# Letting the tile scheduler order three engines in the dense stages of a two-layer hybrid step, with kept output weights and a two-deep chain of sums

## The chip, the cores and the metric

The kernel runs on one core of a Trainium2 chip. The metric is the device time of one execution in microseconds (us). TensorE (PE) multiplies, VectorE (DVE) and ScalarE (ACT) do the elementwise work, GpSimd (POOL) some sums, and SyncE (SP) issues most DMAs.

## The reference, cut to what matters

One inference step over 1024 latent tokens and 256 context tokens, width 1024, in two layers. Layer 0 mixes tokens with a bidirectional S5 scan, layer 1 with grouped-query attention; a SwiGLU FFN of inner width 2816 follows each.

```
for layer in range(2):
    h = modulate(x, shift1, scale1)
    m = s5_mixer(h) if layer == 0 else attention(h)      # s5: scan, gelu, GLU, w_out; attention: qkv, softmax, w_o
    x = layer_norm(ALPHA * x + gate1 * m)
    h = modulate(x, shift2, scale2)
    f = (silu(h @ w_gate) * (h @ w_up)) @ w_out
    x = layer_norm(ALPHA * x + gate2 * f)
```

All arithmetic keeps fp32 accuracy.

## The kernel before

**Layout.** Activations lie feature-major: 8 feature tiles of 128 rows, with the tokens in three chunks: c=0 and c=1 of 512 latent tokens, c=2 of 256 context tokens. Nearly everything lies in one pool of 88 pages of 128x512 fp32 (and 12 half pages).

**Split products.** A matrix product is three matmuls: each fp32 operand is split into a high part (a rounding copy on ScalarE) and a low part (a subtraction on VectorE), and high-high, high-low and low-high are accumulated in PSUM. Weights come by SP's DMA into three raw buffers (`wr`) and are split a half tile at a time (`w_ahead`, lines 102 and 103; for the gated products `i_step`, lines 914, 919 and 923).

**Gated products** (`ffn_step`): the S5 GLU (8 tiles) and the FFN inputs (22 tiles in each layer). The two latent chunks are treated as a 2x2 block product in Winograd's way with 7 block products P1 to P7, each of 12 matmuls of 128x512 (line 961). They need differences of the input h: T1, T2, T3, T4 (`x_next`: a subtraction on line 852, the high part on 855, the low part on 856), and the plain splits B11, B21, B22 (lines 830 and 831). G and U are the context chunk's products, 24 matmuls of 128x256 each (line 971). A *head* of a tile is what needs only chunk 0 (P1, P2) and chunk 2 (G, U); a *tail* is the rest. Five tiles of each gated product start as heads, because chunk 0 is normalised first; their tails follow. P1 ends in a ScalarE copy (line 977), P2 in a VectorE add (981) and the activation (982). The result is spilled to DRAM.

**Output products** (`out_chunks`): 8 output tiles f, contracted over nk=8 tiles (S5 output, attention output w_o) or nk=22 (FFN output), in passes over chunks. `TWO` is first chunks 0 and 2 and then chunk 1; `ONE`, only after the last FFN, is chunk 0, chunk 1, chunk 2. Weights are loaded and split anew in each pass. VectorE accumulates (line 631). In the last pass's f=7 a list of hooks prepares the next stage.

**Boundary** (`cross`, `boundary`, `layer_norm`): the layer norm of a chunk is a generator that yields estimated durations (`YW`). `boundary` weaves its steps by an estimated clock between the units of matmul work: first the output pass of the next chunks, then the heads. A factor `YS`=1.4 stretches the steps, so that they come later. A layer norm subtracts the mean (line 698), squares on ScalarE (700), sums the 8 squares with 7 VectorE adds (702 and 706), sums over features by a matmul with a column of ones (711), takes a reciprocal square root on VectorE, spreads it (691), multiplies (718), makes the modulated h (727) and the residual (752), which ScalarE's own DMA queue stores. After chunk 1's layer norm come, still in the boundary, all of T1, T2, T3, T4 and B22 (`x_rest`), one after the other.

**Order of the instructions.** Everything stands under `tc.manual_schedule()`: each engine issues its instructions in the order in which the Python code emits them. Without it, the tile framework's scheduler would pick, for each engine, the order by simulating the program: of the instructions that are ready at a simulated moment it takes the one that was emitted first. Either way the order is fixed at build time and each engine works through its own list.

Of the kernel before, what the change touches and what calls it, by code (L numbers as in the profile page):

```python
# [6 lines left out]
F32 = mybir.dt.float32  # L7
# [8 lines left out]
KT = 8  # L16
# [597 lines left out]
class Dense(S5):  # L614
# [63 lines left out]

    def layer_norm(self, acc, c, cols, raw, ready, after=None, then=()):

# [16 lines left out]
        for kt in range(KT):  # L697
            v.tensor_tensor(acc[kt][c], acc[kt][c], pm, op=ALU.subtract)
            q[kt] = self.pgn(n)
            nc.scalar.activation(q[kt], acc[kt][c], AF.Square)  # L700
            if kt > 2:
                v.tensor_tensor(q[0], q[0], q.pop(kt - 2), op=ALU.add)
            if kt in (2, 5):
                yield YW[1] * n / 512
        for kt in range(KT - 2, KT):
            v.tensor_tensor(q[0], q[0], q.pop(kt), op=ALU.add)
        yield YW[2] * n / 512 + YW[3]

        ps = self.psum()
        for t in range(nt):  # L710
            mm(ps[:, t:t + 1], q[0][:, 128 * t:128 * t + 128], self.ones[:, 0:1], start=True, stop=True)
        rstd = self.small.tile([P, 4], F32, tag="rstd", name=self.nm("rstd"))[:, :nt]
# [42 lines left out]

    def boundary(self, outs, passes, ln, heads, ready, slow=1.0):

        gens = []
        self.rs = {}
        clock = [0.0, 0.0]  # L760

        def step():
            t = next(gens[0], None)
            if t is None:
                gens.pop(0)
                t = YW[0]
            return t * slow

        def run(units):

            for u in units:
                clock[0] += u() or 0.0
                while gens and clock[0] >= clock[1]:
                    clock[1] = max(clock[1], clock[0] - 2.0) + step()

        for units, cs in zip(outs, passes):
            run(units)
            if not gens:
                clock[1] = clock[0] + YW[0]
            gens += [ln(c, ready) for c in cs]  # L780
        for c, units in heads or ():
            while not ready[c]:
                clock[1] = clock[0] + step()
            run(units)
        lap = 0
        while gens:

            for g in [gens[-1]] * (2 if lap == 3 else 1) + gens[-2::-1]:
                if next(g, 0) == 0:
                    gens.remove(g)  # L790
            lap += 1
# [17 lines left out]

YT, YS = 1.8, 1.4  # L810

# [3 lines left out]
class Ffn(Dense):  # L815

    def x_start(self, raw):
        self.xr = raw
        self.hs = {}
        self.X = {n: [None] * 4 for n in ("B11", "B21", "B22", "T1", "T2", "T3", "T4")}  # L820
        self.xt = {}
        self.xq = {"B11": 0, "B21": 0, "B22": 0, "T1": 0, "T2": 0, "T3": 0, "T4": 0, "C": 0}
# [11 lines left out]
    def x_next(self, n):  # L834

        nc, r = self.nc, self.xr
        v = nc.vector
        k = self.xq[n]
        if k == (8 if n == "C" else 4):
            return False  # L840
        self.xq[n] += 1
        if n == "C":
            self.h_split(k, 2, v)
        elif n[0] == "B":
            kt, c = k + 4 * (n[1] == "2"), int(n[2]) - 1
            self.h_split(kt, c, v)
            self.X[n][k] = self.hs[kt, c]
        else:
            t = self.page()
            x, y = {"T1": lambda: (r[k][1], r[k][0]), "T2": lambda: (r[k + 4][1], self.xt["T1", k]),  # L850
                    "T3": lambda: (r[k + 4][1], r[k][1]), "T4": lambda: (r[k + 4][0], self.xt["T2", k])}[n]()
            v.tensor_tensor(t, x, y, op=ALU.subtract)
            self.xt[n, k] = t
            hi, lo = self.page(F32R), self.page(F32R)
            nc.scalar.activation(hi, t, AF.Copy)
            v.tensor_tensor(lo, t, hi.bitcast(F32), op=ALU.subtract)
            self.X[n][k] = hi, lo
        return True

    def x_all(self, *names):  # L860
        for n in names:
            while self.x_next(n):
                pass

    def x_rest(self, *names):

        for n in names or ("T1", "T2", "T3", "T4", "B22"):
            while self.x_next(n):
                yield YT


# [66 lines left out]
    def ffn_step(self, i, kind, act):  # L938
# [39 lines left out]
        elif kind == "P2":  # L978
            B = product("B", True)
            x = e["s1"] = self.page() if head else e["s1"]  # L980
            v.tensor_tensor(x, e["s2"] if head else x, B, op=ALU.add)
            ac(x, x, act)
        elif kind == "P5":
# [51 lines left out]
    def ffn_body(self, act, last):  # L1035
        for i in range(self.nhead, len(self.segs)):
            for s, kind in enumerate(self.segs[i][1][1]):
                if i == len(self.segs) - 1:
                    last(s)
                self.ffn_step(i, kind, act)  # L1040
        self.X = self.hs = self.xr = self.xt = self.ev = None

# [37 lines left out]

    def out_chunks(self, acc, gate, nk, passes, residual, scale=None, hook=()):

# [9 lines left out]
        def unit(p, f, lo):  # L1092
            cs = passes[p]
            hi = min(lo + 8, nk)
            if lo == 0:
                st["ps"] = [self.psum()[:, :CH[c][1]] for c in cs]
                for c in cs:
                    if f == 0:
                        load(c, 0)
                    if f < 7:  # L1100
                        load(c, f + 1)
            w = self.w_next()
            base = sum(nk * len(x) for x in passes[:p])
# [391 lines left out]


NHP = 12, 88

# [3 lines left out]
class Full(Attn):  # L1502
    def run(self):
        tc, nc, I = self.tc, self.nc, self.I
        with ExitStack() as st:
            st.enter_context(tc.manual_schedule())
            dp = st.enter_context(tc.tile_pool(name="dram", bufs=1, space=bass.MemoryType.DRAM))
# [20 lines left out]
            self.pages.release()  # L1528
            self.pp.release()

    def rows(self, n, *ix):
        return [self.I[n][ix + (i,)] for i in range(self.I[n].shape[len(ix)])]

    def rest(self):
# [30 lines left out]


        self.wpools.append(tc.alloc_tile_pool(name="w2", bufs=1, side="left", reuse_waits="tile"))
        zz = new()
# [25 lines left out]
        self.out_start(KT, TWO, self.spilled)  # L1594
        self.wseq += self.out_plan(L("w_s5_out"), KT, 2)
        self.LS = 1.5
# [7 lines left out]
        def ffn(l, cols, outs, acc, passes):  # L1604

            raw = self.xr
            self.cross(outs, TWO, acc, cols, raw, ready, self.ffn_heads(AF.Silu), keep, self.x_rest())
            self.out_start(NF, passes, self.spilled)
# [8 lines left out]

        outs = lambda: self.out_chunks(acc, self.mod(0, 2), KT, TWO, inputs, ALPHA, ffn_hook(0))

# [26 lines left out]
        acc = None  # L1646
        self.LS = 2
        self.at_queries(hh, hl)
        hh = hl = self.hs = self.xr = None
        self.wseq += self.out_plan(L("w_o"), KT, 2)  # L1650
        self.LS = 1.5
# [3 lines left out]
        ahead.update({(2 + k // 3, 2 * (k % 3)): [lambda k=k: self.z_ahead(2 * k + 2, 0)] for k in range(6)})  # L1655
        self.attention(ahead)
        self.apool.release()
        acc = new()
        hook = ffn_hook(1)
        outs = self.out_chunks(acc, self.mod(1, 2), KT, TWO, self.residual, None, hook)  # L1660

# [6 lines left out]
    def cross(self, outs, passes, acc, cols, raw, ready, heads, after, then=()):  # L1668
        ready[:] = [False] * 3
        self.boundary(outs, passes, lambda c, ready: self.layer_norm(acc, c, cols, raw, ready, after, then if c == 1 else ()),  # L1670
                      heads, ready, YS if then else 1.0)

# [367 lines left out]
```

## Time and profile before

| | |
|---|---|
| median of 3 runs | 3472.22 us (3468.31 to 3476.12) |
| the profiled execution | 3475.9 us, span 3474.1 us |
| PE busy | 3198.7 us, 92% |
| DVE, ACT, POOL busy | 2109.9 us, 1401.9 us, 274.5 us |
| mean granted TensorE clock | 0.957 of full |

Busy is the time in which an engine has an instruction at work. Matmuls are pipelined, so the duration of one is longer than the time from one to the next. The clock is the share of full speed that was granted to TensorE. The span is the time from the first to the last instruction of the core; the time of a run also holds what lies around it.

### The profile page before, as it was taken

What the parts mean: (1) busy time and instruction counts of PE and PEld (TensorE: products, weight loads), DVE (VectorE), ACT (ScalarE), POOL (GpSimd) and SP (SyncE); (2) the same over time, 40 slices, a digit from 0 to 9 for tenths busy, and PEclk for the clock granted to TensorE, in tenths of its full rate; (3) what the DMA queues carried; (4) which work ended last, traced back from release to release, by engine and by line L of the source; (5) the groups of instructions that cost most, each with busy time, mean ns of one, the idle gap of its engine ahead of it and who ended that gap; (6) DMA issues with size and microseconds to landing.
All of it is one profiled execution on the core that took longest, in us unless ns stands there. A gap on an engine that the chain in (4) does not pass through costs nothing. (4 is left out here: it accounts for less than half of the span.)

```text
span 3474.1 us, 46877 instructions
## 1 busy us (share of the span) xinstructions
PE 3198.7 (92%) x17674; PEld 2675.3 (77%) x17674; DVE 2109.9 (61%) x4381; ACT 1401.9 (40%) x2740; POOL 274.5 (8%) x286
## 2 busy tenths in 40 slices
PE   8989659997699999999989999999859999999997
PEld 5753648886478888888878899998647888888776
DVE  7899646556664444524566888885666444453645
ACT  3351433336422222413543577773552222232433
POOL 1230100010000000010012310001000000000001
PEclk9999779998799999999999999999879999999998
DMA  7679942343122121624421100103322222244544
GB/s 257 171 222 323 239 126 85 100 153 114 65 83 77 61 78 61 205 65 139 140 93 57 61 21 16 35 1 101 106 72 85 75 73 66 73 156 133 172 126 137
DMA packets 229971, 384.04 MB, mean 111 GB/s; under 512 B 54688, under 2 KB 111296, under 8 KB 228976
## 3 DMA queue, kind: packets, MB, share of 16 engines
q1 hardware_dynamic: 208720, 335.12, 30.7%
q0 software_dynamic: 7632, 25.35, 2.4%
q10 hardware_dynamic: 13392, 20.58, 1.6%
q8 instruction: 138, 2.26, 0.3%
q14 instruction: 89, 0.73, 0.1%
HBM read 300.23 MB, written 80.74 MB: 110 GB/s over the span
## 5 line engine op out<-in xcount | busy, mean ns | idle before, releaser
L961 PE MATMUL ps<-pg,pg 128*128 128x512 f32 x4368 | 1050.4, 399 | 121.3 <-ACT pg L919 61.7
L961 PEld LDWEIGHTS ps<-pg,pg 128*128 128x128 f32 x4368 | 830.2, 192 | 310.6 <-ACT pg L919 71.8
L121 PE MATMUL ps<-pg,pg 128*128 128x512 f32 (+1 forms) x1872 | 641.5, 365 | 37.6 <-ACT pg L131 17.4
L123 PE MATMUL ps<-pg,pg 128*128 128x512 f32 (+1 forms) x1872 | 634.5, 361 | 4.1 <-DVE pg L132 3.6
L125 PE MATMUL ps<-pg,pg 128*128 128x512 f32 (+1 forms) x1872 | 629.6, 359 | 0.2 <-DVE pg L103 0.2
L121 PEld LDWEIGHTS ps<-pg,pg 128*128 128x128 f32 x1872 | 350.2, 192 | 103.8 <-ACT pg L131 22.2
L123 PEld LDWEIGHTS ps<-pg,pg 128*128 128x128 f32 x1872 | 350.1, 192 | 63.4 <-DVE pg L132 9.9
L125 PEld LDWEIGHTS ps<-pg,pg 128*128 128x128 f32 x1872 | 349.2, 191 | 54.1 <-DVE pg L103 2.1
L971 PEld LDWEIGHTS ps<-pg,pg 128*128 128x128 f32 x2496 | 318.7, 195 | 23.8 <-ACT pg L830 14.4
L971 PE MATMUL ps<-pg,pg 128*128 128x256 f32 x2496 | 322.1, 286 | 14.8 <-ACT pg L830 13.8
L102 ACT ACTIVATE pg<-wr 128x512 fp32r<-128x512 f32 x344 | 191.8, 597 | 356.4 <-DMA wr<-in_w_ffn_out 163.8
L103 DVE TENSOR_TENSOR pg<-wr,pg 128x512 fp32r<-128x512 f32 x344 | 259.1, 793 | 125.8 <-ACT pg L102 114.4
L631 DVE SCALAR_TENSOR_TENSOR pg<-ps,mods,pg 128x512 f32<-128x512 f32 x64 | 47.9, 749 | 274.0 <-PE ps L125 269.4
L923 DVE TENSOR_TENSOR pg<-wr,pg 128x512 fp32r<-128x512 f32 x232 | 158.1, 685 | 41.9 <-ACT pg L919 41.9
L132 DVE TENSOR_TENSOR pg<-ps,pg 128x512 fp32r<-128x512 f32 (+1 forms) x210 | 141.8, 676 | 62.1 <-ACT pg L131 56.8
L919 ACT ACTIVATE pg<-pg 128x512 fp32r<-128x512 f32 x208 | 129.8, 625 | 119.3 <-DVE pg L914 110.7
L1126 POOL TENSOR_TENSOR pg<-pg,pg 128x512 f32<-128x512 f32 x8 | 10.6, 1330 | 1863.4 <-DVE pg L631 1119.7
L1376 ACT ACTIVATE pg<-ps,nb,rq 128x512 f32<-128x512 f32 x192 | 148.9, 777 | 5.4 <-DVE sm L1385 2.4
L131 ACT ACTIVATE pg<-ps 128x512 fp32r<-128x512 f32 (+1 forms) x210 | 123.8, 591 | 65.9 <-PE ps L1396 47.6
L919 ACT ACTIVATE pg<-wr 128x512 fp32r<-128x512 f32 x232 | 137.6, 620 | 28.2 <-DMA wr<-in_w_s_glu 14.7
L923 DVE TENSOR_TENSOR pg<-pg,pg 128x512 fp32r<-128x512 f32 x208 | 142.3, 685 | 0.2
L1015 ACT ACTIVATE pg<-pg 128x512 f32<-128x512 f32 x52 | 32.9, 632 | 262.6 <-DVE pg L1014 262.6
(337 smaller groups left out, 4543.1 us busy)
## 6 DMA issues: line engine op xcount, KB each, us to landing
wr<-in_w_ffn_in SPq DMA_DIRECT2D x104, 512.0 KB, 3.6
gw<-in_w_mod SPq DMA_DIRECT2D x192, 256.0 KB, 5.1
wr<-in_w_ffn_out SPq DMA_DIRECT2D x80, 512.0 KB, 3.9
dI<-pg SPq DMA_DIRECT2D x104, 256.0 KB, 4.6
pg<-dI SPq DMA_DIRECT2D x104, 256.0 KB, 5.2
wr<-in_w_ffn_out SPq DMA_DIRECT2D x40, 384.0 KB, 3.9
dX<-pg ACTq DMA_DIRECT2D x48, 256.0 KB, 2.0
pg<-dX SPq DMA_DIRECT2D x48, 256.0 KB, 4.0
```

Source lines behind the costliest of these rows:

```text
L102: nc.scalar.activation(hi, x, AF.Copy)
L103: nc.vector.tensor_tensor(lo, x, hi.bitcast(F32), op=ALU.subtract)
L121: mm(ps[c], wh, rh[c], start=first, stop=False)
L123: mm(ps[c], wh, rl[c], start=False, stop=False)
L125: mm(ps[c], wl, rh[c], start=False, stop=last)
L131: self.nc.scalar.activation(hi, src, AF.Copy)
L132: self.nc.vector.tensor_tensor(lo, src, hi.bitcast(F32), op=ALU.subtract)
L919: nc.scalar.activation(hi, self.isum[i, name], AF.Copy)
L923: v.tensor_tensor(lo, self.isum[i, name], hi.bitcast(F32), op=ALU.subtract)
L961: mm(e[bank], p[:, o], q, start=(first and k == 0 and j == 0), stop=(k == 3 and j == 2), skip_group_check=True)
L971: mm(ps, p[:, o], q, start=(k == 0 and j == 0), stop=(k == KT - 1 and j == 2))
L1376: nc.scalar.activation(p, u["bank"].pop((qt, kc)), AF.Exp, bias=nb[:, 0:1], scale=rq, accum_out=sm[:, kc:kc + 1])
```

## The change

The whole mixer of layer 0 (with the scan) and the queries and attention of layer 1 stay in the emitted order on every engine. In the other stages only SP and GpSimd keep it; the order of TensorE, VectorE and ScalarE is the scheduler's.

- The output products with nk=8 (S5 output and w_o) load and split their weights once, keep all 8 split tiles (4 pages each) through the first pass, and give them back in the second.
- `x_next` puts off the low part of a T until the next T's subtraction has been emitted. In the FFN boundaries `x_rest` makes only T1 and T2; T3, T4 and B22 are made inside the first tail, after P6, P5 and P7.
- In a head, P2 accumulates in P1's PSUM bank, and the activation reads the bank: the add on line 981 goes for heads.
- `layer_norm` gets `short`: no VectorE adds of squares; TensorE sums all 8 squares with the column of ones (8 accumulating matmuls for each 128 tokens in place of one). It is used for chunk 1 of the two FFN-entry boundaries and for chunk 2 of the last layer norm.
- The stretch factor becomes 0.5 during the output passes and 0.8 during the heads (`YS`), and `YT` goes from 1.8 to 1.4.

```diff
@@ layer_norm
-            q[kt] = self.pgn(n)
+            q[kt] = self.page()[:, :n] if short else self.pgn(n)
...
-            if kt > 2:
+            if kt > 2 and not short:
                 v.tensor_tensor(q[0], q[0], q.pop(kt - 2), op=ALU.add)
...
-            mm(ps[:, t:t + 1], q[0][:, 128 * t:128 * t + 128], self.ones[:, 0:1], start=True, stop=True)
+            for kt in sorted(q):
+                mm(ps[:, t:t + 1], q[kt][:, 128 * t:128 * t + 128], self.ones[:, 0:1], start=(kt == 0), stop=(kt == max(q)))
@@ boundary
-            return t * slow
+            return t * pace[last[0]]
@@
-YT, YS = 1.8, 1.4
+YT, YS = 1.4, (0.5, 0.8)
@@ x_next
-            hi, lo = self.page(F32R), self.page(F32R)
+            self.x_flush()
+            hi = self.page(F32R)
             nc.scalar.activation(hi, t, AF.Copy)
-            v.tensor_tensor(lo, t, hi.bitcast(F32), op=ALU.subtract)
-            self.X[n][k] = hi, lo
+            def rest():
+                lo = self.page(F32R)
+                v.tensor_tensor(lo, t, hi.bitcast(F32), op=ALU.subtract)
+                self.X[n][k] = hi, lo
+            self.xlo.append(rest)
...
+    def x_flush(self):
+        for f in self.xlo:
+            f()
+        self.xlo = []
@@ ffn_step
         elif kind == "P2":
-            B = product("B", True)
-            x = e["s1"] = self.page() if head else e["s1"]
-            v.tensor_tensor(x, e["s2"] if head else x, B, op=ALU.add)
-            ac(x, x, act)
+            if head:
+                e["s1"] = self.page()
+                ac(e["s1"], product("R", False), act)
+            else:
+                x = e["s1"]
+                v.tensor_tensor(x, x, product("B", True), op=ALU.add)
+                ac(x, x, act)
@@ ffn_body
                 self.ffn_step(i, kind, act)
+                if i == self.nhead:
+                    self.x_all(*{"P6": ("T3",), "P5": ("T4",), "P7": ("B22",)}.get(kind, ()))
@@ out_chunks
-            w = self.w_next()
+            if keep and p:
+                w = st.pop(("w", f))
+            else:
+                w = self.w_next()
+                if keep:
+                    st["w", f] = w
@@ run, rest
-            st.enter_context(tc.manual_schedule())
+            self.guard = None
+            self.order()
...
+KEEP = {mybir.EngineType.SP, mybir.EngineType.Pool}
...
+        self.guard = self.tc.manual_schedule(engines=engines) if engines else self.tc.manual_schedule()
...
+        self.order(KEEP)
...
-        self.wseq += self.out_plan(L("w_s5_out"), KT, 2)
+        self.wseq += self.out_plan(L("w_s5_out"), KT, 1)
...
+        self.order()
         self.at_queries(hh, hl)
...
         self.attention(ahead)
+        self.order(KEEP)
@@ cross
-        self.boundary(outs, passes, lambda c, ready: self.layer_norm(acc, c, cols, raw, ready, after, then if c == 1 else ()),
-                      heads, ready, YS if then else 1.0)
+        self.boundary(outs, passes, lambda c, ready: self.layer_norm(acc, c, cols, raw, ready, after, then if c == 1 else (),
+                                                                                    c == passes[-1][0] and (then != () or heads is None)),
+                      heads, ready, YS if then else (1.0, 1.0))
```

## Rows read from the trace of the kernel before

**Rows 1.** The page's busy time, and PEclk by 40 slices.
```profile
PE 3198.7 (92%) x17674; PEld 2675.3 (77%) x17674; DVE 2109.9 (61%) x4381; ACT 1401.9 (40%) x2740; POOL 274.5 (8%) x286
PEclk9999779998799999999999999999879999999998
```

**Rows 2.** Windows: stretch, length; busy PE, PEld, DVE, ACT, POOL; clock; DMA share, GB/s.
```profile
457.36:545.00 87.64, 63.91 (x241) 50.06 (x242) 52.80 (x89) 35.86 (x65) 0.00 (x0) 0.80 0.32 84
768.60:812.40 43.80, 42.02 (x191) 34.19 (x189) 30.81 (x55) 21.36 (x35) 7.77 (x6) 1.00 0.34 116
812.40:931.90 119.50, 67.86 (x317) 54.39 (x317) 78.31 (x161) 71.95 (x129) 0.00 (x0) 0.74 0.24 80
931.90:1437.60 505.70, 499.82 (x2616) 429.97 (x2617) 255.45 (x416) 146.11 (x269) 0.00 (x0) 1.00 0.24 79
...
2481.00:2602.50 121.50, 68.81 (x317) 55.70 (x317) 78.38 (x161) 71.43 (x128) 0.00 (x0) 0.76 0.23 78
...
3236.50:3369.00 132.50, 126.23 (x547) 102.23 (x546) 65.93 (x115) 46.30 (x86) 9.33 (x6) 0.96 0.44 141
3369.00:3452.50 83.50, 68.86 (x522) 67.04 (x520) 50.50 (x97) 36.81 (x69) 5.99 (x6) 0.90 0.52 161
3452.50:3474.10 21.60, 2.88 (x10) 2.16 (x10) 10.87 (x38) 6.13 (x13) 3.44 (x6) 0.62 0.15 49
```

**Rows 3.** The chain that ended last, in FFN 1's body: start, us, what.
```profile
2736.52 13.63 PE ps L961 x60
2750.15 2.87 PE ps L971 x24
```

**Rows 4.** TensorE's timeline at FFN 0's entry: start, us, work [idle before, releaser].
```profile
812.19 0.39 PE L125 MATMUL ps<-pg,pg 128*128 128x512 f32 x1
817.50 1.22 PE L961 MATMUL ps<-pg,pg 128*128 128x512 f32 x2 [4.92 <-ACT pg L919]
...
840.51 1.01 PE L711 MATMUL ps<-ones,hp 128*128 128x1 f32 x4 [3.17 <-DVE hp L706]
...
852.12 8.26 PE L971 MATMUL ps<-pg,pg 128*128 128x256 f32 x48 [6.90 <-ACT pg L830]
...
881.29 1.05 PE L711 MATMUL ps<-ones,pg 128*128 128x1 f32 x8 [0.45 <-DVE pg L706]
...
904.15 12.15 PE L961 MATMUL ps<-pg,pg 128*128 128x512 f32 x24 [16.45 <-ACT pg L855]
931.91 4.63 PE L961 MATMUL ps<-pg,pg 128*128 128x512 f32 x12 [15.61 <-ACT pg L919]
```

**Rows 5.** VectorE's timeline at the same place.
```profile
813.32 4.90 DVE L831 TENSOR_TENSOR pg<-pg,pg 128x512 fp32r<-128x512 f32 x8 [4.03 <-ACT pg L830]
...
832.32 1.08 DVE L698 TENSOR_TENSOR hp<-hp,ps 128x256 f32<-128x256 f32 x3
...
898.16 0.69 DVE L856 TENSOR_TENSOR pg<-pg,pg 128x512 fp32r<-128x512 f32 x1 [0.69 <-ACT pg L855]
...
900.15 0.69 DVE L856 TENSOR_TENSOR pg<-pg,pg 128x512 fp32r<-128x512 f32 x1 [0.70 <-ACT pg L855]
```

**Rows 6.** Weight splits on VectorE in the S5 output's second pass.
```profile
L103 DVE TENSOR_TENSOR pg<-wr,pg 128x512 fp32r<-128x512 f32 x11 | 7.2, 687 | 5.3 <-ACT pg L102 5.3
```

**Rows 7.** Groups by line and shape, whole span: busy us, mean ns | idle before.
```profile
L102 ACT ACTIVATE pg<-wr 128x512 fp32r<-128x512 f32 x304 | 179.0, 622 | 339.4 <-DMA wr<-in_w_ffn_out 163.8 <-PE ps L123 59.8 <-DMA wr<-in_w_o 41.7
...
L981 DVE TENSOR_TENSOR pg<-pg,ps 128x512 f32<-128x512 f32 x52 | 35.7, 687 | 143.4 <-PE ps L961 143.4
...
L977 ACT ACTIVATE pg<-ps 128x512 f32<-128x512 f32 x52 | 30.9, 594 | 80.6 <-PE ps L961 80.4
L702 DVE TENSOR_TENSOR pg<-pg,pg 128x512 f32<-128x512 f32 x40 | 30.4, 759 | 0.1
...
L702 DVE TENSOR_TENSOR hp<-hp,hp 128x256 f32<-128x256 f32 x20 | 8.4, 422 | 0.0
```

**Rows 8.** Line 961 on TensorE at the S5 GLU's start: min/median/max ns.
```profile
L961 PE MATMUL ps<-pg,pg x193: 387/393/795, 457.4 to 545.0; 128*128 128x512 f32 x193
```

More of the change, by code (lines that the diff above doesn't have):

```diff
@@ L677, in rsqrt, with layer_norm @@
             v.scalar_tensor_tensor(out if it == 2 else y, t, 1.5, y, op0=ALU.add, op1=ALU.mult)
-    def layer_norm(self, acc, c, cols, raw, ready, after=None, then=()):
+    def layer_norm(self, acc, c, cols, raw, ready, after=None, then=(), short=False):
         nc = self.nc
@@ L704, in layer_norm @@
                 yield YW[1] * n / 512
-        for kt in range(KT - 2, KT):
-            v.tensor_tensor(q[0], q[0], q.pop(kt), op=ALU.add)
-        yield YW[2] * n / 512 + YW[3]
+        if not short:
+            for kt in range(KT - 2, KT):
+                v.tensor_tensor(q[0], q[0], q.pop(kt), op=ALU.add)
+        yield YW[2] * n / 512 + YW[3] * (0.5 if short else 1.0)
         ps = self.psum()
         for t in range(nt):
-            mm(ps[:, t:t + 1], q[0][:, 128 * t:128 * t + 128], self.ones[:, 0:1], start=True, stop=True)
+            for kt in sorted(q):
+                mm(ps[:, t:t + 1], q[kt][:, 128 * t:128 * t + 128], self.ones[:, 0:1], start=(kt == 0), stop=(kt == max(q)))
         rstd = self.small.tile([P, 4], F32, tag="rstd", name=self.nm("rstd"))[:, :nt]
@@ L754, in affine, with boundary @@
             after(nc.scalar, kt, c)
-    def boundary(self, outs, passes, ln, heads, ready, slow=1.0):
+    def boundary(self, outs, passes, ln, heads, ready, pace=(1.0, 1.0)):
         gens = []
@@ L774, in run @@
                     clock[1] = max(clock[1], clock[0] - 2.0) + step()
+        last = [0]
         for units, cs in zip(outs, passes):
@@ L780, in boundary @@
             gens += [ln(c, ready) for c in cs]
+        last[0] = 1
         for c, units in heads or ():
@@ L820, in x_start @@
         self.X = {n: [None] * 4 for n in ("B11", "B21", "B22", "T1", "T2", "T3", "T4")}
-        self.xt = {}
+        self.xt, self.xlo = {}, []
         self.xq = {"B11": 0, "B21": 0, "B22": 0, "T1": 0, "T2": 0, "T3": 0, "T4": 0, "C": 0}
@@ L863, in x_all @@
                 pass
+        self.x_flush()
     def x_rest(self, *names):
@@ L869, in x_rest @@
                 yield YT
+        self.x_flush()
     def i_start(self, win, pairs, first):
@@ L1079, in z_ahead, with out_chunks @@
             self.zk += 1
-    def out_chunks(self, acc, gate, nk, passes, residual, scale=None, hook=()):
+    def out_chunks(self, acc, gate, nk, passes, residual, scale=None, hook=(), keep=False):
         v, g = self.nc.vector, self.nc.gpsimd
@@ L1529, in run, with order @@
             self.pp.release()
+            self.guard.__exit__(None, None, None)
+    def order(self, engines=None):
+        if self.guard:
+            self.guard.__exit__(None, None, None)
+        self.guard = self.tc.manual_schedule(engines=engines) if engines else self.tc.manual_schedule()
+        self.guard.__enter__()
     def rows(self, n, *ix):
@@ L1606, in ffn @@
             raw = self.xr
-            self.cross(outs, TWO, acc, cols, raw, ready, self.ffn_heads(AF.Silu), keep, self.x_rest())
+            self.cross(outs, TWO, acc, cols, raw, ready, self.ffn_heads(AF.Silu), keep, self.x_rest("T1", "T2"))
             self.out_start(NF, passes, self.spilled)
@@ L1616, in ffn_hook @@
             return some(0, ("B11", "B21"), 8) + [lambda k=k: self.i_until(k) for k in range(6)] + some(2, ("C",), 8)
-        outs = lambda: self.out_chunks(acc, self.mod(0, 2), KT, TWO, inputs, ALPHA, ffn_hook(0))
+        outs = lambda: self.out_chunks(acc, self.mod(0, 2), KT, TWO, inputs, ALPHA, ffn_hook(0), True)
         ffn(0, self.ln_cols(0, 0, 0, 3, 4), outs(), acc, TWO)
@@ L1647, in rest @@
         self.LS = 2
+        self.order()
         self.at_queries(hh, hl)
         hh = hl = self.hs = self.xr = None
-        self.wseq += self.out_plan(L("w_o"), KT, 2)
+        self.wseq += self.out_plan(L("w_o"), KT, 1)
         self.LS = 1.5
@@ L1659, in rest @@
         hook = ffn_hook(1)
-        outs = self.out_chunks(acc, self.mod(1, 2), KT, TWO, self.residual, None, hook)
+        outs = self.out_chunks(acc, self.mod(1, 2), KT, TWO, self.residual, None, hook, True)
         ffn(1, self.ln_cols(1, 0, 1, 3, 4), outs, acc, ONE)
```

## The prediction, as it went on record

> **What bounds the kernel now.** I read the page first: TensorE is busy 92% of the span, VectorE 61%, ScalarE 40%, and the granted clock falls below full in few slices [rows 1]. So time can only be won where TensorE stands still. The windows by stage show where. The body of FFN 0 takes 505.7 us with TensorE busy for 499.8 at full clock [rows 2], and in the chain of waits the body of FFN 1 is matmuls without a gap: 60 of 128x512 in 13.63 us (0.227 each), 24 of 128x256 in 2.87 us (0.120 each), one tile in 84 x 0.227 + 48 x 0.120 = 24.8 us [rows 3]. Nothing is to be had there, and there are 8 + 22 + 22 = 52 such tiles. The loss lies in stretches between: the two FFN entries (812.4 to 931.9 and 2481.0 to 2602.5), the start of the S5 GLU (457 to 545), the last passes of the FFN output (3236.5 to 3452.5) and the end (21.6 us) [rows 2].
>
> Take the first FFN entry. Its matmuls are 10 head products of 12 (120 x 0.227 = 27.3 us), 6 context products of 24 (144 x 0.120 = 17.2), two tail products (5.5) and some 5 us of small layer-norm matmuls (four groups of 1.0 us [rows 4] and the means): 55 us of work in 119.5. The second takes 121.5. So 64.5 and 66.5 us are lost. TensorE's timeline names the waits [rows 4]: 4.9 us after the output's last matmul for the splits of h; 3.2 and 6.9 us (and shorter ones between) for chunk 2's layer norm; 16.5 and 15.6 us for the T chain. VectorE's timeline shows why. Chunk 2's layer norm starts only at 832.3, 20 us after the output has ended, and the B11/B21 splits after it too. The T chain is a ping-pong: 852 subtracts, ScalarE rounds, 856 subtracts, and the next 852 starts only then; a T each 2.0 us (856 at 898.16, at 900.15), of which VectorE idles 0.7 [rows 5]. All 16 T's and B22 stand before the first tail. No engine is full: VectorE 78 us, ScalarE 72 of 119.5. The clock is 0.74 in the stretch: TensorE falls to its lower level when it waits. The 24 matmuls at 904 took 12.15 us, 0.51 each in place of 0.227 [rows 4], so a wait removed gives more than itself.
>
> **The change part by part.** *Earlier layer norms (factor 1.4 to 0.5).* The generator yields (YW) 3 + 3 + 5 + 3.5 + 4 x 1 = 18.5 us until chunk 0 is ready and 6.4 + 2.5 more until chunk 2's turn, from about 3.5 us after the second output pass has begun. At 1.4 chunk 0 was ready at 3.5 + 25.9 = 29 us of a pass of 44, and chunk 2's began at 42. At 0.5 that is 12.8 and 17 us, and chunk 2 (13 us of its own) is ready at 24. Both, and the splits of h in the hooks of f=7, then stand before the end of the pass. What moves out of the entry on VectorE: chunk 2's layer norm 11.6 us, B11/B21 4.9, C 2.8, weight splits 3.1, together 22.4; the 8 residual stores on ScalarE's queue go with it. The work lands in the second pass, where VectorE is busy 30.8 of 43.8 us [rows 2].
>
> *Weights kept.* The second pass loses its splits: 11 low parts on VectorE in this window, 7.2 us [rows 6], the like on ScalarE (0.62 each, rows 7 name the group), and 8 loads of 512 KB on SP's queue, behind which the FFN's first weights then stand earlier. For TensorE alone that is worth nothing, since the pass runs at 96% (42.0 of 43.8 us). Its worth is room: 30.8 - 7.2 + 22.4 = 46 us of VectorE work in 43.8. The pass becomes just full, so a few us spill into the entry. The kept tiles hold 8 x 4 = 32 of 88 pages.
>
> *T chain.* With the low part put off by one, subtract and low part go back to back, at the 0.61 us spacing of eight 831s in 4.9 us [rows 5]: 1.2 us a T. Only T1 and T2 stay, 8 T's in 9.8 us in place of 16 x 2.0 + 4 x 0.61 = 34 us for all T's and B22. T3, T4 and B22 (20 operations, 12 us) come inside the first tail; they issue no DMA. There VectorE has 12 + 12 x 0.61 of weight work + 7 x 0.69 of evacuations = 24 us against 19.4 us of matmuls: a loss of 5 us, given back at each entry.
>
> *Heads' P2.* 15 VectorE adds of 0.69 us go [rows 7]. But P2's first matmul now waits in P1's bank for P1's copy, 0.6 us [rows 7] and some 0.4 us of signalling as I estimate it from the idle times of the same size in rows 5. Behind P2 on TensorE stand the next tile's P1 and G, and for these the evacuations. Unhidden this costs 15 x 1.0 = 15 us; where another tile's P1 is ready, the scheduler can put it between: 0. I take 5.
>
> *Short.* For chunk 1, 7 adds of 0.69 us leave VectorE (the mean of 0.76 in [rows 7] holds a few long ones) and 28 matmuls come: 4 of them took 1.05 us in 8 instructions [rows 4], so 7 us of TensorE, in a stretch where it has gaps. Only the last square's 4 are on the path, as before. At the end of the kernel the 7 adds of 0.42 us [rows 7] sit between the subtractions: -2 us.
>
> *Sum for an entry.* What is left in the stretch on VectorE is 78.3 - 22.4 - 13.8 (20 operations of T3, T4, B22 at 0.69) - 4.8 - 3.4 = 34 us; on ScalarE 72 less the same two groups there (22 and 12 x 0.63) = 42; on TensorE 55 + 7. So TensorE becomes the bound, from below 55 us. I take 70: 55, 7 for the added matmuls, and 8 for the spill and the clock. Gain 119.5 - 70 = 49.5 and 121.5 - 70 = 51.5, less 5 each for the first tail: 91. Bounds: 120 (both waits vanish) and 50 (only the T chain's 22 to 25 us are won).
>
> *Order by the scheduler.* In the entries it is what makes the interleaving above come true. Elsewhere: the S5 GLU's start has 193 matmuls of 128x512 [rows 8] among its 241 [rows 2], so 43.9 + 48 x 0.120 = 49.6 us in 87.6, VectorE 52.8, and the same T chain: 16 T's at 0.8 us less is 13; I take 15 (0 to 30). The last passes of the FFN output, not touched otherwise, need 120.3 + 63.1 us by the same rates, with some 8 us of layer norm, in 132.5 + 83.5: 24.6 us lost; I take 8 (from -5 to 18). The 52 tiles of the bodies I leave as they are: 0 (above 0 nothing, below as in the rival).
>
> Total: 91 + 15 + 8 + 2 - 5 = 111 us. The profiled execution took 3475.9 us, 3.7 over the median of 3472.2, so 3475.9 - 111 = 3365 by the one and 3361 by the other. I forecast 3365 us.
>
> **The rivals.** *1. The order is wrong for the chip (slower).* The order is frozen at build time from simulated durations. Where a simulated engine is quicker or slower than the real one, an instruction that isn't ready stands before one that is, and all behind it wait. The bodies are where this hurts: they have no slack on TensorE. One misplaced pair of split operations costs 0.69 + 0.62 us. Two such in each tile: 52 x 2 x 1.31 = 136 us, and 3365 + 136 = 3501. It decides from 111/52 = 2.1 us a tile. Against it: VectorE is busy 51% and ScalarE 29% there [rows 2], so a wrong order is mostly absorbed by splits made ahead. The Trainium skill's page "PSUM — Partial Sum Buffer" (section Engine vs sequencer instructions) states that these queues are strict FIFO and that matmuls start and complete in program order; the trace agrees, with TensorE idle 16.45 us behind one wait.
>
> *2. Half of it arrives.* The 32 kept pages and the two-deep sums fill the 88 pages; what should run early waits for a free page, or VectorE is overfull in the second pass. Then chunk 2's layer norm is late as before (4.9 + 3.2 + 6.9 us and the short waits, 20 us at each entry) and the rest at the S5 GLU and the FFN outputs is nil: 3365 + 40 + 15 + 0 = 3420.
>
> *3. More arrives.* The entries fall to near 60 us and the last passes lose little: 3365 - 20 - 10 - 10 = 3325.
>
> *4. It nets out.* Scheduler losses of 2 us a tile meet the gain: 3472.
>
> **How the numbers follow.** Forecast (3335 to 3395): 0.52. Half (3395 to 3465): 0.22. More (below 3335): 0.07. Within 0.2% of 3472, about what a measurement of this kernel can tell from no change (7 us): 0.04. Slower: 0.15. So faster 0.81, same 0.04, slower 0.15. The range goes from 3318 to 3475; it leaves out the slower case and the far end of "more". The likeliest case's own range is 3335 to 3395.
>
> **What would show it.** The two entries, from the last output matmul to the third tail product, 70 us each with a clock over 0.9; VectorE nearly full in the second output passes, with no line 103 or its successor there; chunk 2's subtractions before the output's end; T1's low parts 1.2 us apart; the bodies still at 24.8 us a tile. Wrong would be: bodies above 25.5 us a tile (rival 1), chunk 2's layer norm still after the output (rival 2), or TensorE waiting for pages, seen as waits of ScalarE or VectorE on TensorE's or a DMA's reading.

## The result and the profile after

The changed kernel takes 3372.06 us (median of 4 runs, 3369.82 to 3376.47) against 3470.26 us (3465.96 to 3476.12): a ratio of 0.9717, 95% interval 0.9698 to 0.9736. That is 98 us faster; the forecast was 3365 us. The profiled execution took 3376.47 us with a span of 3372.8.

The page's busy times and clock by slices answer to [rows 1]:

```profile
PE 3196.8 (95%) x17814; PEld 2692.5 (80%) x17814; DVE 2057.7 (61%) x4313; ACT 1383.7 (41%) x2708; POOL 266.7 (8%) x286
PEclk9999879998899999999999999999989999999998
```

TensorE is busy for nearly as long as before (3196.8 us for 3198.7) in a span 101 us shorter. The 140 added matmuls are the squares of `short`. (Lines have moved: 961 is now 978, 971 is 988, 711 is 713, 830 and 831 are 834 and 835, 852, 855 and 856 are 856, 861 and 865, 919 and 923 are 936 and 940, 977 is 994.) The windows by stage, columns as in [rows 2]: the S5 output's second pass; FFN 0's entry, from the last output matmul to the third tail product as in [rows 2], and its body; FFN 1's entry; and the last output's second and third pass and the end.

```profile
749.62:802.83 53.21, 49.72 (x217) 40.75 (x215) 34.02 (x66) 26.88 (x46) 7.82 (x6) 0.94 0.21 77
802.83:895.20 92.37, 73.24 (x372) 63.72 (x370) 51.34 (x113) 51.70 (x95) 0.00 (x0) 0.83 0.27 87
895.20:1398.60 503.40, 499.36 (x2618) 430.04 (x2617) 268.39 (x428) 152.74 (x276) 0.00 (x0) 1.00 0.23 77
2427.73:2518.45 90.72, 73.98 (x371) 63.96 (x370) 49.57 (x110) 48.59 (x89) 0.00 (x0) 0.81 0.28 89
...
3146.26:3272.51 126.25, 123.78 (x547) 100.88 (x546) 64.63 (x115) 45.87 (x86) 8.46 (x6) 1.00 0.46 150
3272.51:3350.05 77.54, 71.78 (x547) 69.88 (x545) 49.92 (x99) 35.96 (x69) 4.85 (x6) 0.93 0.49 157
3350.05:3372.80 22.75, 8.64 (x38) 7.74 (x38) 8.30 (x31) 5.51 (x13) 3.45 (x6) 0.58 0.14 46
```

The passes of the last output are cut here at their first matmul. At the same matmuls, the kernel before shows:

```profile
3230.69:3365.75 135.06, 128.79 (x547) 103.86 (x546) 65.93 (x115) 46.30 (x86) 9.33 (x6) 0.96 0.44 143
3365.75:3452.55 86.80, 72.11 (x547) 70.10 (x545) 53.19 (x101) 36.81 (x69) 5.99 (x6) 0.90 0.50 155
```

The two entries fall from 119.5 and 121.5 us to 92.4 and 90.7, with the granted clock up from 0.74 and 0.76 to 0.83 and 0.81. FFN 0's body is nearly as long as before (503.4 us for 505.7). The body's rate is told by the chain of waits, which answers to [rows 3]:

```profile
2625.25 13.63 PE ps L978 x60
2638.88 2.87 PE ps L988 x24
2641.75 5.47 PE ps L978 x24
2647.22 2.87 PE ps L988 x24
```

One tile still takes 13.63 + 2.87 + 5.47 + 2.87 = 24.84 us. TensorE's timeline at FFN 0's entry answers to [rows 4]:

```profile
802.67 0.50 PE L713 MATMUL ps<-ones,hp 128*128 128x1 f32 x4
812.28 1.19 PE L691 MATMUL ps<-ident,rstd 128*128 128x128 f32 x4 [9.12 <-DVE rstd L677]
813.13 10.61 PE L978 MATMUL ps<-pg,pg 128*128 128x512 f32 x36
...
828.15 3.04 PE L978 MATMUL ps<-pg,pg 128*128 128x512 f32 x12 [0.79 <-ACT pg L994]
831.02 0.72 PE L713 MATMUL ps<-ones,pg 128*128 128x1 f32 x6
832.39 1.42 PE L713 MATMUL ps<-ones,pg 128*128 128x1 f32 x6 [0.64 <-ACT pg L700]
834.43 4.61 PE L978 MATMUL ps<-pg,pg 128*128 128x512 f32 x12 [0.62 <-ACT pg L994]
838.88 8.64 PE L713 MATMUL ps<-ones,pg 128*128 128x1 f32 x52
...
889.73 6.65 PE L978 MATMUL ps<-pg,pg 128*128 128x512 f32 x28
...
905.21 8.00 PE L978 MATMUL ps<-pg,pg 128*128 128x512 f32 x24 [3.91 <-ACT pg L834]
```

The two waits of 16 us for the T chain are gone. At 889.73 the first tail starts without a wait: the last head's P2 has just been read (ScalarE's line 998 at 888.50), and VectorE adds P6 of the tail at 892.68. Its P5 and P7 follow, and the 3.91 us stand inside this tail, before its last two products, P4 and P3. Chunk 2's squares are summed right behind the output's last matmul (802.67), where before they came 28 us after it. What stands out is the new wait of 9.12 us in front of chunk 2's spread (691). VectorE's timeline answers to [rows 5]:

```profile
806.94 0.15 DVE L670 TENSOR_SCALAR rs<-ps 128x2 f32<-128x2 f32 x1
807.01 3.08 DVE L940 TENSOR_TENSOR pg<-wr,pg 128x512 fp32r<-128x512 f32 x5
810.02 0.16 DVE L671 TENSOR_SCALAR rs<-rs 128x2 int32<-128x2 int32 x1
...
862.67 0.69 DVE L865 TENSOR_TENSOR pg<-pg,pg 128x512 fp32r<-128x512 f32 x1 [1.18 <-ACT pg L861]
863.89 0.69 DVE L865 TENSOR_TENSOR pg<-pg,pg 128x512 fp32r<-128x512 f32 x1 [0.53 <-ACT pg L861]
...
881.57 0.69 DVE L931 TENSOR_TENSOR pg<-wr 128x512 f32<-128x512 f32 x1 [5.89 <-DMA wr<-in_w_ffn_in]
```

T's low parts now come 1.2 us apart. And five weight splits (940) stand between the first and second step of the reciprocal root that 691 waits for. TensorE's list has 691 ahead of 36 matmuls of head products (813.13), and these wait too. But the low parts of their own first weights are only made from 807.01 on (the same five splits), so the place of 691 in the list can't be worth all of the 9.12 us; an estimate from these rows is 4 to 5. The load of the first tail's weights is a further limit: VectorE waits 5.89 us for it at 881.57, and TensorE, at 882.91, 4.39 us for a weight's low part (940) that stands behind it in VectorE's list. The kernel before had this wait too (3.72 us on VectorE).

**Where the time came from.** The trace cut at the first matmul of each stage, in us, for every kernel of this study ("order", "edits" and so on are explained with the experiments):

| kernel | mixer and GLU | S5 output, FFN 0 | FFN 0 output to keys | scores, attention | w_o, FFN 1 | FFN 1 output to end |
|---|---|---|---|---|---|---|
| before | 694.4 | 743.2 | 437.2 | 488.9 | 745.2 | 365.1 |
| after | 682.2 | 716.4 | 419.8 | 488.9 | 709.7 | 355.7 |
| e1 edits, hand order | 683.1 | 748.2 | 436.7 | 488.9 | 736.9 | 368.1 |
| e2 order only | 686.6 | 726.1 | 421.2 | 488.9 | 719.6 | 355.0 |
| e3 PE kept | 679.5 | 737.2 | 426.6 | 489.0 | 729.4 | 358.8 |
| e4 DVE, ACT kept | 680.9 | 738.9 | 430.8 | 489.0 | 726.4 | 369.0 |
| e5 P2 with add | 682.5 | 704.8 | 421.8 | 488.9 | 698.2 | 355.0 |
| e6 no short | 682.2 | 710.3 | 420.1 | 489.0 | 703.1 | 354.6 |
| e7 old pace | 677.3 | 720.1 | 421.8 | 488.9 | 715.2 | 354.5 |
| e8 no keep | 680.1 | 722.8 | 422.9 | 489.0 | 713.9 | 355.8 |
| e9 both | 677.1 | 703.4 | 419.6 | 489.0 | 694.0 | 354.3 |
| e10 old T chain | 690.3 | 725.1 | 421.3 | 489.0 | 718.8 | 355.6 |
| e11 e9 by hand | 679.8 | 727.0 | 437.4 | 488.9 | 722.3 | 368.7 |
| e12 pace 0.25 | 674.8 | 706.0 | 420.3 | 488.9 | 697.1 | 352.2 |

By spans the change wins 101.3 us. As the table cuts it, 12.2 come up to the S5 output, 26.8 and 35.5 in the two stages that hold the FFN entries, 17.4 from FFN 0's output to the keys, and 9.4 in the last. The last cut doesn't fall at the same work, though. Where TensorE's order is the scheduler's, some first matmuls of the last output (three; two in e4) stand ahead of FFN 1's last 24:

```profile
3017.07 0.40 PE L121 MATMUL ps<-pg,pg 128*128 128x512 f32 x1
...
3017.76 5.61 PE L978 MATMUL ps<-pg,pg 128*128 128x512 f32 x24
```

These 24 take 5.4 us, from 3017.76 to the next output matmul at 3023.21, and the table counts them in the last stage. With them moved back, the two FFN stages win 26.8 and 30.1 us and the last 14.8. The same 5.4 us have to be moved in e2, e5 to e10 and e12 before these two columns are set against the kernel before, e1, e3 or e11. Within the FFN stages the entries win 27.0 and 30.7 us and the bodies some 2 each; the output passes ahead of them lose 2.4 and 3.0.

### The profile page after: what moved, and what is told of

It is laid out like the page before. It is cut to its first block, busy times and chain, and to the rows that moved or that the text cites. A ratio compares the mean times of both kernels' runs of the same rounds, so it can differ in the third digit from the quotient of the medians.

```text
span 3372.8 us, 47213 instructions
## 1 busy us (share of the span) xinstructions
PE 3196.8 (95%) x17814; PEld 2692.5 (80%) x17814; DVE 2057.7 (61%) x4313; ACT 1383.7 (41%) x2708; POOL 266.7 (8%) x286
## 4 chain that ended last, share of the span: by engine, by line
PE 81%; DVE 12%; DMA 3%; ACT 2%; issue 1%; SPq 1%; ACTq 0%; POOL 0%; DVEq 0%; POOLq 0%
PE ps L978 28%; PE ps L121 10%; PE ps L123 10%; PE ps L125 10%; PE ps L988 8%; PE ps L1425 2%; DVE sw L537 1%; PE ps L1445 1%; PE ps L1446 1%; PE ps L1444 1%; PE ps L1383 1%; PE ps L1384 1%; PE ps L1385 1%; DVE X L543 1%; DVE sw L541 1%
## 5 line engine op out<-in xcount | busy, mean ns | idle before, releaser
L978 PE MATMUL ps<-pg,pg 128*128 128x512 f32 x4368 | 1035.8, 395 | 39.1 <-ACT pg L936 22.8
L103 DVE TENSOR_TENSOR pg<-wr,pg 128x512 fp32r<-128x512 f32 (+1 forms) x312 | 219.5, 733 | 189.5 <-ACT pg L102 115.2
L102 ACT ACTIVATE pg<-wr 128x512 fp32r<-128x512 f32 (+1 forms) x312 | 175.4, 596 | 271.2 <-DMA wr<-in_w_ffn_out 89.2
L940 DVE TENSOR_TENSOR pg<-wr,pg 128x512 fp32r<-128x512 f32 x232 | 158.1, 687 | 104.4 <-ACT pg L936 102.5
L936 ACT ACTIVATE pg<-wr 128x512 fp32r<-128x512 f32 x232 | 139.5, 624 | 79.6 <-PE ps L988 37.2
L1390 DVE TENSOR_REDUCE mx<-ps 128x1 f32<-128x512 f32 (+1 forms) x208 | 137.1, 661 | 1.3 <-PE ps L1385 1.3
```

What stands on the lines that cost most here:

```text
L102: nc.scalar.activation(hi, x, AF.Copy)
L103: nc.vector.tensor_tensor(lo, x, hi.bitcast(F32), op=ALU.subtract)
L936: nc.scalar.activation(hi, self.isum[i, name], AF.Copy)
L940: v.tensor_tensor(lo, self.isum[i, name], hi.bitcast(F32), op=ALU.subtract)
L978: mm(e[bank], p[:, o], q, start=(first and k == 0 and j == 0), stop=(k == 3 and j == 2), skip_group_check=True)
L1390: v.tensor_reduce(mx[:, kc:kc + 1], ps, axis=AX.X, op=ALU.max)
```

## The experiments

The theory behind the forecast (A): the edits (earlier layer norms, shorter T chain) take away the waits of the entries, and the scheduler's order adds a little elsewhere. Its rival (B): the order does most. Ratios are against the kernel before, with 95% intervals; differences between kernels are differences of medians. The four medians of the kernel before, one for each set of runs, lie between 3470.3 and 3473.2.

**e1, all edits in the hand-written order.**

```
     def order(self, engines=None):
-        self.guard = self.tc.manual_schedule(engines=engines) if engines else self.tc.manual_schedule()
+        self.guard = self.tc.manual_schedule()
```

> All edits of the text stay, but every engine keeps the emitted order everywhere. Theory A (the edits do most of it: earlier layer norms, two T's instead of four in the boundary, kept weights; the scheduler only fills small waits): 3395 to 3425 us, the two FFN entries some 35 us shorter each than before, the attention's head and the FFN output passes as before. Theory B (the scheduler's order does most of it, the edits are nearly idle without it): 3445 to 3475 us.

3464.73 us, 0.9985 [0.9974, 0.9997]. **e2, the old code with only the order freed** in the same regions (`order(KEEP)` put into the kernel before).

> The kernel before with only the order of PE, VectorE and ScalarE left to the scheduler outside scan and attention; weights split in each pass, all T's in the boundary, one-deep T chain, late layer norms. Theory A: 3430 to 3455 us (only the small waits at the FFN output passes, the S5 GLU and the K/V projection go, some 20 to 40 us). Theory B: 3370 to 3400 us, since an instruction that is ready early is taken early wherever the text has put it.

3399.26 us, 0.9799 [0.9779, 0.9818]. So the edits alone bring 6 us, the order alone 72, both together 98. The theory fell, and the rival stands, for the edits taken together; e11 below shows which of them hide what the others bring. TensorE's timeline of e1 at FFN 0's entry shows why the edits bring nothing by hand:

```profile
822.87 1.22 PE L691 MATMUL ps<-ident,rstd 128*128 128x128 f32 x4 [10.86 <-DVE rstd L677]
...
828.78 5.73 PE L978 MATMUL ps<-pg,pg 128*128 128x512 f32 x24 [0.69 <-ACT pg L994]
...
841.55 8.38 PE L978 MATMUL ps<-pg,pg 128*128 128x512 f32 x24 [6.17 <-ACT pg L994]
850.61 3.01 PE L978 MATMUL ps<-pg,pg 128*128 128x512 f32 x12 [0.69 <-ACT pg L994]
...
884.43 4.73 PE L978 MATMUL ps<-pg,pg 128*128 128x512 f32 x12 [6.53 <-ACT pg L994]
...
902.42 5.49 PE L978 MATMUL ps<-pg,pg 128*128 128x512 f32 x12 [4.76 <-ACT pg L994]
```

The 16 us waits for T are gone here too. In their place are waits for ScalarE's 994 in front of heads' products, 18.8 us, and 10.86 us for chunk 2's root. The order alone (e2), at the same place, still waits 15.74 us for the T chain and 16.62 for a weight's low part, which VectorE makes behind the chain. From the last output matmul to the third tail product it takes 114.8 us, 4.5 less than before; the rest of the 17.1 us that its stage wins lies in the output passes (3.6) and in the body (9.0):

```profile
888.33 8.95 PE L961 MATMUL ps<-pg,pg 128*128 128x512 f32 x24 [15.74 <-ACT pg L855]
...
914.12 2.08 PE L971 MATMUL ps<-pg,pg 128*128 128x256 f32 x8 [16.62 <-DVE pg L923]
```

**e3 and e4: whose freedom counts?** The changed kernel with further engines in `KEEP`.

```
-KEEP = {mybir.EngineType.SP, mybir.EngineType.Pool}
+KEEP = {mybir.EngineType.SP, mybir.EngineType.Pool, mybir.EngineType.PE}                                  # e3
+KEEP = {mybir.EngineType.SP, mybir.EngineType.Pool, mybir.EngineType.DVE, mybir.EngineType.Activation}   # e4
```

> As after, but TensorE too keeps the emitted order; VectorE and ScalarE are the scheduler's. In after TensorE stood 9.1 us at the FFN entry before the spread of chunk 2's reciprocal root (L691), which its list had ahead of heads. If TensorE's own reordering is worth little (theory A): 3365 to 3385 us, or less where the 9 us wait goes. If the gain comes from TensorE jumping over products that are not ready (theory B): 3400 to 3430 us.

> As after, but VectorE and ScalarE keep the emitted order; only TensorE's is the scheduler's. Theory A: near the all-manual run with the edits, 3390 to 3420 us, since the waits are on VectorE's and ScalarE's lists. Theory B with TensorE as the mover: 3375 to 3395 us.

3421.09 us, 0.9858 [0.9844, 0.9873], and 3436.94 us, 0.9903 [0.9888, 0.9917]. Against e1's 3464.73, freeing VectorE and ScalarE alone (e3) is worth 44 us, freeing TensorE alone (e4) 28, and all three 93: more than the 72 of the two by themselves. The stage up to the keys, which the edits leave as it is (e1: 436.7 of 437.2), gains 10.6 by e3, 6.4 by e4 and 17.4 with both. e4 lies above both of its expected ranges.

**e5 to e8, e10: each edit undone under the scheduler.**

```
# e5: P2 of a head as before: a bank of its own and VectorE's add
# e6: the short argument of cross's layer_norm
-  c == passes[-1][0] and (then != () or heads is None)),
+  False),
# e7
-YT, YS = 1.4, (0.5, 0.8)
+YT, YS = 1.8, (1.4, 1.4)
# e8: w_s5_out and w_o planned twice, out_chunks without its last argument True
-        self.wseq += self.out_plan(L("w_o"), KT, 1)
+        self.wseq += self.out_plan(L("w_o"), KT, 2)
# e10
-            self.xlo.append(rest)
+            rest()
...
-  self.x_rest("T1", "T2"))
+  self.x_rest())
```

> As after, but a head's P2 has its own PSUM bank and the VectorE add again (15 adds of 0.69 us back, the wait of P2 for P1's copy gone). In the all-manual run with the edits TensorE waited 19 us at the first FFN entry for that copy (L994); in after the group of L978 shows 3.4 us in all. If the scheduler hides the wait as after's rows say: 3366 to 3376 us. If the shared bank is what still holds the entries: 3350 to 3362.

> As after without the short layer norm: 7 VectorE adds back, 28 small matmuls less for chunk 1 at each FFN entry and 14 less at the end. In after 52 of them took 8.6 us of TensorE in a row at the first entry. If TensorE is the bound there: 5 to 8 us less at each entry, 2 more at the end, 3358 to 3366. If VectorE is: 3374 to 3386.

> As after with the old stretch factors (1.4 throughout, 1.8 a T). If what is ready is taken early wherever the text puts it, the text's place matters only as a priority: 3366 to 3380 us. If the earlier layer norms of the text are needed beside the scheduler: 3390 to 3410, chunk 2's layer norm late again.

> As after, but the S5 output's and w_o's weights are loaded and split again for the second pass (32 splits on each of VectorE and ScalarE, 16 loads of 512 KB). If VectorE's room in the second output pass is what the layer norms need: 5 to 10 us more at each entry, 3382 to 3392. If the 32 kept pages cost as much as the room gives: 3366 to 3376.

> As after, with the T's as before: T1 to T4 and B22 all in the boundary, low part right behind its high part. With the order alone the entries still showed waits of 15.7 and 16.6 us on the T's at the first entry. If the T edit is what the scheduler cannot do by itself: 3395 to 3420. If the scheduler interleaves the T's anyway: 3370 to 3380.

| undone | us | ratio [95%] | the edit is worth |
|---|---|---|---|
| e5, shared bank of P2 | 3349.49 | 0.9644 [0.9629, 0.9660] | -23 |
| e6, short | 3355.94 | 0.9663 [0.9647, 0.9679] | -16 |
| e7, pace | 3378.36 | 0.9732 [0.9714, 0.9750] | +6 |
| e8, kept weights | 3377.70 | 0.9724 [0.9708, 0.9740] | +6 |
| e10, T chain | 3400.68 | 0.9789 [0.9775, 0.9803] | +29 |

The changed kernel was not run again with these sets. By the ratios, each against the kernel before in its own set, the five are worth -25, -19, +5, +2 and +25 us. The ratios of e7 and e8 overlap with that of the changed kernel, so these runs do not tell their +6 from nothing. e6 and e8 lie just outside their expected ranges. The T chain is the edit that pays, by 8.7 and 9.1 us in the stages of the entries and some 8 before the S5 output. This first column moves by some us on its own (last section); from the S5 GLU's first matmul to its end, e10 takes 232.6 us for 221.5. Two edits cost time. e5's timeline, at the same place, shows the first:

```profile
812.20 10.18 PE L978 MATMUL ps<-pg,pg 128*128 128x512 f32 x36
822.22 1.02 PE L695 MATMUL ps<-pg,ones 128*128 128x512 f32 x2
822.67 8.80 PE L978 MATMUL ps<-pg,pg 128*128 128x512 f32 x36
831.31 9.83 PE L713 MATMUL ps<-ones,pg 128*128 128x1 f32 x64
...
894.25 7.55 PE L978 MATMUL ps<-pg,pg 128*128 128x512 f32 x24 [4.25 <-DVE pg L1016]
```

With banks of their own, six products (72 matmuls) run from 812.2 to 831.3, 19.1 us, with no wait between. In the changed kernel they take from 813.1 to 838.9, 25.8 us: three waits of 0.62 to 0.79 us, of which two are for ScalarE's 994, 12 small matmuls in between, and 12 matmuls at 834.43 that took 4.61 us, 0.38 each against 8.80/36 = 0.24; the granted clock was 0.79 from 831 to 839, where e5 had 1.00 from 822.6 to 831.3. The last two products of the first tail start 11 us earlier (894.25 for 905.21), as the stage is 11.6 us shorter, and 11.5 at the second entry. In the S5 GLU, with five heads, nothing is gained.

**e9, P2's add and `short` only in the last layer norm; e11, the same in the hand-written order; e12, e9 with an earlier pace.**

```
# e9, beside e5's edit
-  c == passes[-1][0] and (then != () or heads is None)),
+  c == passes[-1][0] and heads is None),
# e11: e9 with e1's edit.   # e12: e9 with
-YT, YS = 1.4, (0.5, 0.8)
+YT, YS = 1.4, (0.25, 0.8)
```

> As after, with P2's own bank and add in the heads, and short kept only for the last layer norm. If the two losses (22 and 16 us alone) lie in different places, the sum: 3332 to 3340 us. If they are the same TensorE time at the entries, won once: 3345 to 3352.

> The all-manual run with the edits, but with P2's own bank and add and without short for chunk 1. If the bank wait (19 us at the first entry) and the row of small matmuls (9 us) are why the edits gave only 6 us in the hand order: 3405 to 3425. If the hand order itself is the limit: 3440 to 3460.

> As e9, with the first stretch factor 0.25 for 0.5. TensorE's list then has chunk 2's mean and spread 73 matmuls or more ahead of the heads, and the waits of 9.1 and 7.4 us before that spread should go, with some of the low clock after them: 15 to 20 us under e9. If VectorE's second pass is the limit, the wait only moves into the pass: within 5 us of e9.

e9 takes 3337.16 us, 0.9609 [0.9596, 0.9622]: 35 us better than the changed kernel, of 38.7 for e5 and e6 added, so the two costs are nearly separate. It is the best version of the study. e11 takes 3424.87 us, 0.9857 [0.9844, 0.9871]: by hand the better edits bring 48 us where those of the change bring 6, and the freed order adds another 88. So by hand the shared bank and `short` cost 40 us, about what they cost under the scheduler (35), and the edits without them bring 48 us by hand and 62 under the scheduler (e9 against e2). The edits were not idle in the hand-written order; two of them ate what the others brought. e12 takes 3342.98 us, 0.9625 [0.9612, 0.9638], no better than e9. The timelines of e9 and then e12 around FFN 0's entry:

```profile
807.17 1.19 PE L691 MATMUL ps<-ident,rstd 128*128 128x128 f32 x4 [9.11 <-DVE rstd L677]
...
832.80 1.83 PE L713 MATMUL ps<-ones,pg 128*128 128x1 f32 x8 [4.87 <-DVE pg L707]
...
887.11 7.97 PE L978 MATMUL ps<-pg,pg 128*128 128x512 f32 x24 [4.26 <-ACT pg L834]
```

```profile
759.42 1.87 PE L713 MATMUL ps<-ones,pg 128*128 128x1 f32 x8 [5.42 <-DVE pg L707]
...
785.66 1.01 PE L713 MATMUL ps<-ones,hp 128*128 128x1 f32 x4 [6.53 <-DVE hp L707]
...
793.89 0.61 PE L691 MATMUL ps<-ident,rstd 128*128 128x128 f32 x4
...
886.83 8.65 PE L978 MATMUL ps<-pg,pg 128*128 128x512 f32 x24 [4.91 <-ACT pg L834]
```

In e12 chunk 2's spread (691 of 4 matmuls, 793.89) stands inside the second output pass, without a wait. But the wait has only moved into that pass: TensorE stands there 5.42 and 6.53 us for the sums of squares of chunks 0 and 2, and its last output matmul ends at 810.85 in place of 797.72. The entry behind it is as much shorter (65.6 us to the third tail product for 79.4), and the last two products of the first tail start at 886.83, as in e9 (887.11). That is the second branch of the recorded expectation, within 5 us of e9: the 9.1 us wait, the largest left in e9, is not won by an earlier pace alone.

## Why the prediction was right, and where its steps were not

The forecast of 3365 us is within 7 us of the median, and the likeliest case (3335 to 3395) came. That is in part luck: its terms erred by 18 and 17 us, and some others, in opposite directions, and 6 us of the closeness come from the time that the gain was taken from, the profiled execution of 3475.9 us and not the median of 3470.3.

- **P2's bank wait: the mis-sized term.** Priced at 5 us, at most 15; measured 23 us, 11.6 and 11.5 at the two entries with five heads each, and nothing in the S5 GLU. The step supposed a wait of 1 us that another tile's P1 might fill. What the runs showed is a stretch of products broken by waits of 0.6 to 0.8 us and slowed matmuls behind them, with the end of the first tail late by 11 us.
- **The two entries, -91.** The sign named for this, 70 us each with a clock over 0.9, did not come: 92.4 and 90.7 us, at 0.83 and 0.81. With P2's 5 taken off, 86 us were forecast, and the two stages won 26.8 + 30.1 = 56.9. Without the shared bank (e5) they win 38.4 + 41.6 = 80.0, so P2 explains 23 of what is missing from 91 and leaves 11; e5's entries still take 82.4 and 79.9 us, with the 9.12 us wait of the first in them.
- **Short: the right size.** 7 us of TensorE for each entry stood inside the 70; undoing it wins 6.1 and 6.6 us there. The 64 matmuls took 9.83 us in e5, 0.15 each. What the step did not see is that this makes the edit a loss: the 4.8 us of VectorE that it saves are worth less. Without it (e9) TensorE does wait 4.87 us for the last of these adds, but then has 8 small matmuls of 1.83 us in place of 64.
- **Order by the scheduler elsewhere: the missed term.** From FFN 0's output to the keys the forecast had nothing; 17.4 us came, and e2 shows 16.0 from the order alone. The groups of TensorE from chunk 1's mean (695) to the keys, before and then after, show one part:

```profile
L121 PE MATMUL ps<-pg,pg 128*128 128x512 f32 (+1 forms) x88 | 27.4, 370 | 7.4 <-ACT pg L830 7.4
...
L711 PE MATMUL ps<-ones,pg 128*128 128x1 f32 x8 | 1.1, 253 | 3.6 <-DVE pg L706 3.6
```

```profile
L121 PE MATMUL ps<-pg,pg 128*128 128x512 f32 (+1 forms) x88 | 27.3, 370 | 4.8 <-ACT pg L834 4.8
...
L713 PE MATMUL ps<-ones,pg 128*128 128x1 f32 x8 | 1.1, 253 | 1.1 <-DVE pg L707 1.1
```

  The waits for the splits of h fall from 7.4 to 4.8 us and for the squares from 3.6 to 1.1; this part of the stage goes from 103.9 to 95.5 us, the part before it, mostly the output passes, from 333.3 to 324.3.
- **GLU start and last stage.** 15 us forecast, 12.2 to 15.8 measured (mixer and GLU together, or the GLU by itself: the mixer's end moves by up to 10 us between profiles). The last stage: 8 + 2 forecast, 14.8 measured. Its second and third pass win 8.8 and 9.3 us, twice the 8 forecast; its first loses 2; and the end, where `short` was to save 2 us, takes 1.2 longer.
- **The sum.** 86 + 15 + 0 + 10 = 111 us forecast; 56.9 + 12.2 + 17.4 + 14.8 = 101.3 measured. P2's miss of 18 us and the 17 us found elsewhere nearly cancel: the total is closer than its parts.
- **What earns the gain.** The steps priced the entries by what the edits take away and the order as what makes that come true. The order is worth more than that: alone it wins 17.1 and 20.2 us in the two stages. The edits by themselves lose 5.0 us in the first and win 8.3 in the second (e1); without P2's bank and `short` they win 16.2 and 22.9 (e11).
- **T chain.** Its low parts are 1.2 us apart, as forecast. T3 and T4 are made inside the first tail, as forecast, between 893 and 904, behind P6's sum; TensorE has P5, P7 and the tail's G to do meanwhile and stands still only 3.91 us, where 5 were to be given back.
- **VectorE full in the second pass.** It is not: 34.02 us busy of 53.21, though line 103 is gone from there and chunk 2's subtractions stand before the output's end (791.95). Chunk 2's root and its splits spilled into the entry, where the 9.12 and 7.39 us waits for the root stand. The root is late although VectorE has room, so the sum of busy times was not what decided it.
- **Rivals.** Rival 1's mechanism exists (a list fixed at build time, with an unready instruction ahead of ones that are ready sooner: 691 in front of 36 matmuls), but at the entries only; the bodies have kept 24.84 us a tile. The rule of the Trainium skill's page "PSUM — Partial Sum Buffer" (section Engine vs sequencer instructions), that matmuls start in program order, agrees with the 9.12 us. Of rival 2 (no free pages) the timelines read here show nothing: the waits in them are for computed splits and roots, and for a load of weights (5.89 us).

**Open.** How the gain of 9 us in the output passes between FFN 0 and the queries divides into single waits was not followed: TensorE's busy time there fell from 325.1 to 317.9 us for the same matmuls, at a clock of 0.98 and then 0.99. What decides when the first tail's weights are loaded was not tried. How much of the entries' gain is the higher clock and how much the waits was not taken apart. Why P2's shared bank costs nothing in the S5 GLU and 11.5 us at an FFN entry was only argued: the waits seen add up to a few us, and the rest stands in later, differently ordered work. Keeping the splits (940) out of the root's steps by themselves was not tried; e12 moved the whole layer norm.

## What to carry to other kernels

Undo each edit by itself, and under the order that will be used. All edits together brought 6 us by hand and 27 under the scheduler; without the two that cost time they bring 48 and 62. The sum of five edits hid that two of them were losses. Try the freed order early: it alone brought 72 us here, more than any edit. Don't let one product continue in the PSUM bank that another engine must first copy, where TensorE is the bound: an add saved on an engine busy 61% of the span cost 23 us, all of it at the two FFN entries and none in the S5 GLU. A total that comes out right says little of its terms: compare stage by stage.

## What the runs showed of the hardware that was not expected

A subtraction on VectorE took 2.6 times as long while GpSimd worked. In the S5 output's second pass of the changed kernel, on GpSimd's and then VectorE's timeline:

```profile
798.98 1.34 POOL L1157 TENSOR_TENSOR pg<-pg,pg 128x512 f32<-128x512 f32 x1 [2.15 <-DVE pg L631]
```

```profile
799.08 1.79 DVE L835 TENSOR_TENSOR pg<-pg,pg 128x512 fp32r<-128x512 f32 x1
...
801.13 0.68 DVE L835 TENSOR_TENSOR pg<-pg,pg 128x512 fp32r<-128x512 f32 x1
```

The same operation takes 1.79 us beside GpSimd's sum and 0.68 without it: 1.1 us more, which is about what was left of that sum. The Trainium skill's page "SBUF — State Buffer" (section Who interferes with whom) states that a VectorE instruction with two SBUF inputs contends with a GpSimd instruction that reads SBUF; this row agrees.

The scan mixer, whose code and order are the same in all these kernels, took 438.6 to 449.1 us in their profiles; why was not looked into. Differences of a few us in the first column of the stage table are therefore not read as effects.
